# Linear attention's level products issued upwards behind the diagonals, with more steps between producer and consumer

## The chip, the cores and the metric

The kernel runs on one core of one Trainium2 chip. The metric is the device time of one execution in microseconds (us), here the median of the runs. The core's engines each work through their own instruction queue in order: TensorE (PE) multiplies, VectorE (DVE) and ScalarE (ACT) do element-wise work, GpSimd (POOL) does little here, and SyncE (SP) issues most of the DMA transfers. An instruction that waits holds back everything behind it on its engine.

## The reference

One decoder layer on 256 tokens of width 2048, in float32. The part that the change touches is the mixer:

```python
n = rms_norm(x, attn_norm_g)
proj = n @ w_in                       # 5672 columns, split into the parts below
gla_out = gla_mixer(gq, gk, gv, g_lr, g_out, ...)     # 4 heads, linear attention with decay
nsa_out = nsa_mixer(nq, kc, vc, ks, vs, kw, vw, ng, ...)   # 8 heads: compressed, selected, window
h = x + jnp.concatenate([gla_out, nsa_out], axis=-1) @ w_out
m = rms_norm(h, ffn_norm_g)
return h + (jax.nn.silu(m @ w_gate) * (m @ w_up)) @ w_down

# in gla_mixer, per head (b is the running sum of the log decay):
decay = jnp.exp(jnp.where(causal, b[:, :, :, None, :] - b[:, :, None, :, :], -jnp.inf))
scores = jnp.einsum('bhtd,bhsd,bhtsd->bhts', qi, ki, decay)
# in nsa_mixer, for the compressed keys and values:
jax.nn.silu(flat @ w1) @ w2
```

## The kernel before

**Products and side work.** The large projections are main work on PE: `proj` (the input projection, 512 columns of `w_in` at a time), `w_out_half` (the output projection, one half of its rows at a time), then the feed-forward part. Each float32 product is done as three matmuls of 512 columns (line 283) on a high and a low part of both operands; lines 137 (ACT) and 138 (DVE) split the weights into `hi` and `lo` as they arrive. Everything else is written as generators ("side work") whose `yield`s mark steps. `drive(mains, pace)` issues the main products, and for each `pace` units of them (a step of three matmuls counts 2) it advances the side work by one step. The pace is 2.5 in the stage of the change and 2 in `w_out_half(0)`. Side work stands in two queues, `urgent` first and then `later`, in which one step goes to the first item in line. `later` holds in order `gla_gate`, `gla_mix`, `compress` (put in at index 1) and `nsa_mix`. So an added `yield` in one of them delays all that comes behind it in `later` by one step of main work. `urgent` and `later` are drained after `w_out_half(0)`. A background generator, `sum_rows` (line 1042), prepares sums of the feed-forward weights on DVE. The program is a Tile program: a scheduler fixes at build time the order of the instructions on each engine, beginning from the order in which the code issues them.

**Linear attention.** `gla_mix` computes two pairs of heads. `gla_decay(hp)` prepares pair `hp`: for each of the seven `LEVELS` 1, 2, 4, ... 64 two tiles of decayed keys and queries (exponentials on ACT, lines 542 and 544; then on DVE the running sums, lines 548 and 550, and the multiplications, lines 552 and 555; level 1 has a copy on line 554), and at the end a tile `off` (lines 560 to 564) for the block of scores between the two halves of the sequence. The running sums go upwards: each level's lines 548 and 550 use what the level before left. `gla_scores(h)` does ten PE products of 128x128 for head `h` (line 581): one for each level, two on the undecayed keys and queries (`near` and `far`, whose diagonals are wanted), and one on `off`. They lie four to a PSUM bank; DVE then merges a bank's products into one score tile by masked copies (`pick`, line 576). `gla_out` (lines 604 to 622) multiplies the scores with the values and normalises.

In `gla_mix` the second pair's decay runs step by step beside the first two heads' scores:

```python
nxt = gla_decay(1)
for h in range(4):
    if h == 2:
        yield from nxt
    for _ in gla_scores(h, res[h]):
        yield
        next(nxt, None)
```

**Compression.** `compress` runs twice, for keys (`w == 0`) and values. The products of line 766 fill a bank, DVE copies it (`hs`), PE transposes it (line 210), DVE reduces it (line 773), ACT applies silu (line 774), and after five further steps PE multiplies the result with the second weights (line 779 for keys, 795 for values). ACT also copies scores of the compressed branch there: lines 638 and 829 (ACT) and 639 (DVE) split the transposed queries. `nsa_mix` follows; its outputs (`put_mix`) must be there before `w_out_half(1)`, which multiplies them.

Of the kernel before, what the change touches and what calls it, by code (L numbers as in the profile page):

```python
# [12 lines left out]
ALU = mybir.AluOpType  # L13
# [15 lines left out]
WARM = (3, 2, 1)  # L29
LINE = 256  # L30
LEVELS = (1, 2, 4, 8, 16, 32, 64)
MASKED = LEVELS[:-1]
M_UP, M_LOW = len(MASKED), len(MASKED) + 1
C_LR, C_GO, C_NQ, C_KC, C_KS, C_KW, C_NG = 2048, 2064, 3088, 4112, 4624, 5136, 5648

# [2 lines left out]
def kernel(  # L38
# [6 lines left out]
    TT, TS, STT = nc.vector.tensor_tensor, nc.vector.tensor_scalar, nc.vector.scalar_tensor_tensor  # L45
# [157 lines left out]
    ident = kp.tile([P, P], F32, name="ident")  # L203
# [187 lines left out]

    lmask = cp.tile([P, len(MASKED) + 2, P], F32, name="lmask")
    cneg = cp.tile([P, 2, P], BF16, name="cneg")
# [8 lines left out]
    def constants():  # L402
# [3 lines left out]
        affine(lmask[:, M_LOW, :], [[-1, P]], -1, 1)  # L406
        for li, l in enumerate(MASKED):

# [117 lines left out]
    def gla_decay(hp):  # L526

        e = dec[hp] = {}

        def cut(a, l):  # L530
            return a.rearrange("p b h (n r i) -> p (b h n) r i", r=2, i=l)

        def blocks(a):
            return a.rearrange("p (b n) i -> p b n i", b=2)

        f_, r_ = (dec[name].rearrange("p c s -> p (c s)").rearrange("p (g b h s) -> p g b h s", g=2, b=2, h=2)[:, hp] for name in "fr")
        k_, q_ = kk[:, hp], qq[:, hp]
        for l in LEVELS:
            e[l] = g2([2, 2, P])
            f, r, q, k, ev = (cut(a, l) for a in (f_, r_, q_, k_, e[l]))  # L540
            n = f.shape[1]
            act(ev[:, :, 1, :], f[:, :, 1, :], AF.Exp, scale=1.0 / TAU)
            if l > 1:
                act(ev[:, :, 0, :], r[:, :, 0, :], AF.Exp, scale=1.0 / TAU)
            yield
            yield
            to, ends = blocks(r[:, :, 0, :]), blocks(f[:, :, 1, l - 1:l])[:, ::-1]
            TT(to, to, ends.to_broadcast([P, 2, n // 2, l]), ALU.add)
            if 2 * l < P:
                TT(f[:, :, 1, :], f[:, :, 1, :], f[:, :, 0, l - 1:l].to_broadcast([P, n, l]), ALU.add)  # L550
            if l > 1:
                TT(ev[:, :, 0, :], ev[:, :, 0, :], k[:, :, 0, :], ALU.mult)
            else:
                nc.vector.tensor_copy(ev[:, :, 0, :], k[:, :, 0, :])
            TT(ev[:, :, 1, :], ev[:, :, 1, :], q[:, :, 1, :], ALU.mult)
            yield
            yield
        off, first_g = g2([2, 2, P]), small([2, 1])
        e["off"] = off
        TS(first_g, f_[:, 0, :, 0:1], 1.0 / TAU, None, ALU.mult)  # L560
        act(off[:, 0], r_[:, 0], AF.Exp, scale=1.0 / TAU)
        for h in range(2):
            act(off[:, 1, h], r_[:, 1, h], AF.Exp, scale=1.0 / TAU, bias=first_g[:, h])
        TT(off, off, k_, ALU.mult)
        yield

    def gla_scores(h, res):

        e, hh, hp = dec[h // 2], h % 2, h // 2
        near, far = kk[:, hp, :, hh], qq[:, hp, :, hh]  # L570
        (sc0, sc1), (sc, sof) = ((t[:, 0], t[:, 1]) for t in (g1([2, P]), g1([2, P])))
        todo = [(e[l][:, 0, hh], e[l][:, 1, hh]) for l in LEVELS[::-1]]
        todo += [(near[:, 0], far[:, 1]), (far[:, 0], near[:, 1]), (e["off"][:, 0, hh], e["off"][:, 1, hh])]

        def pick(to, m, src):
            nc.vector.copy_predicated(to, lmask[:, m, :].bitcast(mybir.dt.uint32), src)

        for at in range(0, len(todo), 4):
            p = bank()
            for j, (u, w) in enumerate(todo[at:at + 4]):  # L580
                mm(p[:, j * P:(j + 1) * P], u, w, start=True, stop=True)  # L581
                yield
            for j in range(len(todo[at:at + 4])):
                i, pl = at + j, p[:, j * P:(j + 1) * P]
                if i == 0:
                    nc.vector.tensor_copy(sc, pl)
                elif i <= len(MASKED):
                    pick(sc, len(MASKED) - i, pl)
                elif i == len(MASKED) + 1:
                    TT(sc0, pl, ident, ALU.mult)  # L590
                    pick(sc0, M_UP, sc)
                elif i == len(MASKED) + 2:
                    TT(sc1[:, ::-1], pl, ident, ALU.mult)
                    pick(sc1[:, ::-1], M_LOW, sc)
                else:
                    act(sof[:, ::-1], pl, AF.Copy)
        res["s"] = sc0, sc1, sof

    def gla_out(h, res):
# [44 lines left out]
    def gla_mix():  # L644
        res = [{} for _ in range(4)]
        yield from gla_decay(0)
        nxt = gla_decay(1)
        for h in range(4):
            if h == 2:
                yield from nxt  # L650
            for _ in gla_scores(h, res[h]):
                yield
                next(nxt, None)
            if h:
                yield from gla_out(h - 1, res[h - 1])
        for _ in range(7):
            yield
        yield from gla_out(3, res[3])
# [73 lines left out]
    def compress():  # L732

        uT = st["uT"]

        def rows_of(i):

            res = []
            for j in range(2):
                to, j0 = g4([8, P]), (i % 2 * 2 + j) * 1024  # L740
                nc.gpsimd.dma_start(to, (k_w1, v_w1)[i // 2][0, j0:j0 + 1024, :].rearrange("(j p) h -> p j h", p=P))
                res.append(to)
            return res

        nxt = rows_of(0)
        for w in range(2):
            ph = bank()
            nc.vector.memset(ph[:, :P], 0.0)
            for half in range(2):
                j0 = 16 * half  # L750
                r = nxt
                if 2 * w + half < 3:
                    nxt = rows_of(2 * w + half + 1)
                blk = g2([16, 2, NCMP])
                for h in range(2):
                    u = uT[:, w, h, j0:j0 + 240].rearrange("p (n j) -> p j n", j=16)
                    TT(blk[:, :, h, :], u, pos[:, w, j0:j0 + 16].unsqueeze(2).to_broadcast([P, 16, NCMP]), ALU.add)
                for _ in range(9):
                    yield
                for j in range(16):  # L760
                    g = 32 * (j % 4)
                    mm(ph[g:g + N2, :P], blk[:, j].rearrange("p h n -> p (h n)"), r[j // 8][:, j % 8, :], start=(half == 0 and j < 4),
                       stop=(half == 1 and j >= 12), tile_position=(0, g), skip_group_check=True)
                    if j % 16 == 15:
                        yield
            hs = g1([P])
            nc.vector.tensor_copy(hs, ph[:, :P])
            for _ in range(6):
                yield
            pt = bank()  # L770
            transpose(pt[:, :P], hs)
            hid = g1([32])
            nc.vector.tensor_reduce(hid, pt[:, :P].rearrange("p (g m) -> p m g", g=4), AX.X, ALU.add)
            act(hid, hid, AF.Silu)
            for _ in range(5):
                yield
            pk = bank()
            if w == 0:
                mm(pk[:N2, :P], hid[:, :N2], cw2[:, 0, :], start=True, stop=True)
                ss = small([1])  # L780
                junk = g1([P])
                act(junk[:N2], pk[:N2, :P], AF.Square, accum_out=ss[:N2])
                TS(ss[:N2], ss[:N2], 1.0 / 128, EPS, ALU.mult, ALU.add)
                rk = small([1])
                rsqrt_(rk[:N2], ss[:N2])
                kk = g1([P])
                TS(kk[:N2], pk[:N2, :P], rk[:N2], None, ALU.mult)
                for _ in range(25):
                    yield
                pt = bank()  # L790
                transpose(pt[:, :N2], kk[:N2, :], N2)
                TS(kcm, pt[:, :N2], kgain[:, 0:1], None, ALU.mult)
            else:
                for h in range(2):
                    mm(pk[:NCMP, h * P:(h + 1) * P], hid[:, h * NCMP:(h + 1) * NCMP], cw2[:, 1, :], start=True, stop=True)
                in_parts(vcm[0][:NCMP], vcm[1][:NCMP], pk[:NCMP, :S].rearrange("p (h d) -> p h d", h=2))
            yield

    nq, sc = {}, {}
# [573 lines left out]
```

## Time and profile before

| | |
|---|---|
| runs (us) | 1122.27, 1120.46, 1120.99; median 1120.99 |
| profiled execution (us) | 1120.81, of which span 1118.8 |
| PE busy | 1100.5 us, 98% of the span |
| DVE busy | 995.1 us, 89% |
| ACT busy | 742.0 us, 66% |
| POOL busy | 76.0 us, 7% |
| DMA | 259.61 MB, mean 232 GB/s |

A row of the profile's timeline gives the start, the duration, the engine, the source line, the operation, the tiles (output<-inputs) and their shape; a bracket at its end gives the idle time before the instruction and the instruction that ended it. Matmuls are pipelined, so the distance between two starts is what one costs, not its listed duration. "PEclk" is the share of full speed that TensorE's clock was granted. Each float32 matmul of line 581 is counted as two in the trace's counts (x14 is seven products).

### The profile page before, as it was taken

What the parts mean: (1) busy time and instruction counts of PE and PEld (TensorE: products, weight loads), DVE (VectorE), ACT (ScalarE), POOL (GpSimd) and SP (SyncE); (2) the same over time, 40 slices, a digit from 0 to 9 for tenths busy, and PEclk for the clock granted to TensorE, in tenths of its full rate; (3) what the DMA queues carried; (4) which work ended last, traced back from release to release, by engine and by line L of the source; (5) the groups of instructions that cost most, each with busy time, mean ns of one, the idle gap of its engine ahead of it and who ended that gap; (6) DMA issues with size and microseconds to landing.
All of it is one profiled execution on the core that took longest, in us unless ns stands there. A gap on an engine that the chain in (4) does not pass through costs nothing.

```text
span 1118.8 us, 14633 instructions
## 1 busy us (share of the span) xinstructions
PE 1100.5 (98%) x5298; PEld 903.7 (81%) x5298; DVE 995.1 (89%) x1277; ACT 742.0 (66%) x1009; POOL 76.0 (7%) x139
## 2 busy tenths in 40 slices
PE   9999996999999999999999999999999999999998
PEld 8878885898777887888878888888888788888886
DVE  6678779878599787998899999999999999999997
ACT  7645556544566487767586676768686776767684
POOL 5110000023110000010000000000000000000000
PEclk9999998999999999999999999999999999999999
DMA  7999984468754675686565747657665657567763
GB/s 268 340 338 363 359 282 138 157 231 302 248 213 165 242 244 177 234 306 226 174 216 194 254 160 254 226 198 242 202 215 202 230 177 257 196 237 235 239 229 113
DMA packets 124850, 259.61 MB, mean 232 GB/s; under 512 B 6709, under 2 KB 8793, under 8 KB 124778
## 3 DMA queue, kind: packets, MB, share of 16 engines
q1 hardware_dynamic: 113514, 219.86, 57.6%
q0 software_dynamic: 10368, 37.75, 9.2%
q10 hardware_dynamic: 896, 1.07, 0.3%
q8 instruction: 41, 0.67, 0.2%
q14 instruction: 31, 0.25, 0.1%
HBM read 239.78 MB, written 18.87 MB: 231 GB/s over the span
## 4 chain that ended last, share of the span: by engine, by line
PE 78%; DVE 11%; DMA 3%; ACT 3%; issue 3%; POOL 1%; ACTq 0%; SPq 0%; POOLq 0%; DVEq 0%
PE bank L283 41%; PE bank L1110 28%; DVE ftwo L639 5%; PE bank L210 3%; PE bank L1251 2%; DMA raw<-in_w_in_dram 2%; DVE lo L138 2%; DVE g L1141 1%; DMA fraw<-in_w_down_dram 1%; PE bank L909 1%; PE bank L581 1%; ACT ftwo L638 1%; PE bank L846 1%; DVE g L639 1%; DVE fsum L1142 1%
## 5 line engine op out<-in xcount | busy, mean ns | idle before, releaser
L1110 PE MATMUL bank<-ftwo,g 128*128 128x512 f32 x1848 | 432.3, 393 | 0.3 <-ACT ftwo L638 0.2
L1110 PEld LDWEIGHTS bank<-ftwo,g 128*128 128x128 f32 x1848 | 342.3, 188 | 77.4 <-DVE ftwo L639 4.3
L283 PE MATMUL bank<-hi,g 128*128 128x512 f32 (+1 forms) x1088 | 320.0, 375 | 0.1
L639 DVE TENSOR_TENSOR ftwo<-fraw,ftwo 128x1536 fp32r<-128x1536 f32 (+1 forms) x130 | 257.9, 1984 | 9.4 <-ACT ftwo L638 8.0
L638 ACT ACTIVATE ftwo<-fraw 128x1536 fp32r<-128x1536 f32 (+1 forms) x130 | 216.9, 1670 | 34.7 <-DMA fraw<-in_w_up_dram 24.7
L283 PE MATMUL bank<-ftwo,g 128*128 128x512 f32 x960 | 221.7, 391 | 0.5 <-ACT bank L1222 0.5
L283 PEld LDWEIGHTS bank<-hi,g 128*128 128x128 f32 x1088 | 192.1, 188 | 31.0 <-ACT hi L323 0.7
L283 PEld LDWEIGHTS bank<-ftwo,g 128*128 128x128 f32 x960 | 179.2, 188 | 40.3 <-ACT bank L1222 2.8
L137 ACT ACTIVATE hi<-raw 128x1024 fp32r<-128x1024 f32 (+3 forms) x124 | 130.7, 1057 | 103.9 <-PE bank L283 78.1
L283 PE MATMUL bank<-lo,g 128*128 128x512 f32 (+3 forms) x544 | 193.7, 375 | 0.2 <-DVE lo L324 0.2
L138 DVE TENSOR_TENSOR lo<-raw,hi 128x1024 fp32r<-128x1024 f32 (+3 forms) x124 | 150.2, 1218 | 37.8 <-ACT hi L137 37.1
L638 ACT ACTIVATE ftwo<-g 128x1024 fp32r<-128x1024 f32 x74 | 78.2, 1056 | 70.0 <-DVE g L1141 43.8
L283 PEld LDWEIGHTS bank<-lo,g 128*128 128x128 f32 x544 | 98.3, 188 | 15.8 <-DVE lo L324 0.6
L639 DVE TENSOR_TENSOR ftwo<-g,ftwo 128x1024 fp32r<-128x1024 f32 x74 | 90.3, 1220 | 10.7 <-ACT ftwo L638 10.7
L639 DVE TENSOR_TENSOR ftwo<-fsum,ftwo 128x1024 fp32r<-128x1024 f32 x74 | 90.2, 1219 | 0.0
L638 ACT ACTIVATE ftwo<-fsum 128x1024 fp32r<-128x1024 f32 x74 | 77.5, 1048 | 5.9 <-DVE fsum L1143 4.7
L1234 ACT COPY g<-bank 128x512 f32<-128x512 f32 x80 | 45.9, 588 | 39.9 <-PE bank L283 38.1
L1141 DVE TENSOR_TENSOR g<-fraw 128x1024 f32<-128x1024 f32 x56 | 67.5, 1219 | 0.0
L1222 ACT COPY bank<-g 128x512 f32<-128x512 f32 x80 | 45.2, 593 | 13.4 <-DVE f L1171 12.1
L638 ACT ACTIVATE g<-bank 128x512 fp32r<-128x512 f32 (+1 forms) x50 | 29.1, 593 | 32.0 <-PE bank L210 27.1
L1099 POOL DMA_DIRECT2D g<-sums x16 | 8.5, 531 | 512.0 <-DVE ftwo L639 482.9
L210 PE MATMUL bank<-ident,g 128*128 128x128 f32 (+2 forms) x214 | 39.0, 278 | 0.9 <-ACT g L478 0.5
(241 smaller groups left out, 909.3 us busy)
## 6 DMA issues: line engine op xcount, KB each, us to landing
fraw<-in_w_gate_dram SPq DMA_DIRECT2D x86, 512.0 KB, 3.9
fraw<-in_w_down_dram SPq DMA_DIRECT2D x42, 1024.0 KB, 5.0
raw<-in_w_in_dram SPq DMA_DIRECT2D x36, 1024.0 KB, 7.4
fraw<-in_w_up_dram SPq DMA_DIRECT2D x70, 512.0 KB, 4.7
sums<-g POOLq DMA_DIRECT2D x32, 512.0 KB, 6.3
raw<-in_w_out_dram SPq DMA_DIRECT2D x16, 1024.0 KB, 5.2
g<-in_w_gate_dram SPq DMA_DIRECT2D x16, 512.0 KB, 7.3
g<-in_w_up_dram SPq DMA_DIRECT2D x16, 512.0 KB, 8.3
```

What stands on the lines that cost most here:

```text
L137: act(h[:, i:i + n], r[:, k + i:k + i + n], AF.Copy)
L138: last["d"] = TT(o[:, i:i + n], r[:, k + i:k + i + n], f32(h[:, i:i + n]), ALU.subtract)
L210: return nc.tensor.transpose(o, i, ident[:n, :n])
L283: last["mm"] = mm(bk[t], a[:, k, t * P:(t + 1) * P], m[:, off:off + w], start=(first_ and k == 0 and i == 0), stop=(end and k == 3 and i = ...
L581: mm(p[:, j * P:(j + 1) * P], u, w, start=True, stop=True)
L638: act(hi, ps, AF.Copy)
L639: last["d"] = TT(lo, ps, f32(hi), ALU.subtract)
L1110: mm(banks[q], x, m, start=todo[q] == total[q], stop=todo[q] == 1)
L1141: TT(s1, r[:, 1:3], r[:, 3:4].to_broadcast([P, 2, 512]), ALU.add)
L1222: nc.scalar.copy(banks[qs[n][t]], h_sb[n][:, t, :])
L1234: nc.scalar.copy(h_sb[n][:, t, :], bs[t])
L1251: mm(bk, u, m, start=(first and i == 0), stop=(end and i == 2), skip_group_check=onto)
```

## The change

Three things. First, `gla_scores` issues `near` and `far` first, then the levels from 1 to 64, then `off`; before, it went from level 64 down to 1, then `near`, `far` and `off`. The picks follow: level 1 is copied whole, the levels 2 to 64 are picked over it, and the merge of the diagonals stands at the end. There are as many picks, copies and multiplications per head as before. Secondly, `gla_mix` takes four empty steps between the first pair's decay and head 0, and begins the second pair's decay at head 1 instead of head 0 (the rest of it still in front of head 2). Thirdly, `compress` takes nine steps instead of five between silu and the second product. Below line 644 the line numbers of the changed kernel are 4 higher (774 becomes 778, 779 783, 795 799, 1042 1046). All lines of the diff:

```diff
@@ -29,7 +29,7 @@
 WARM = (3, 2, 1)
 LINE = 256
 LEVELS = (1, 2, 4, 8, 16, 32, 64)
-MASKED = LEVELS[:-1]
+MASKED = LEVELS[1:]
 M_UP, M_LOW = len(MASKED), len(MASKED) + 1
 C_LR, C_GO, C_NQ, C_KC, C_KS, C_KW, C_NG = 2048, 2064, 3088, 4112, 4624, 5136, 5648
 
@@ -569,8 +569,8 @@
         e, hh, hp = dec[h // 2], h % 2, h // 2
         near, far = kk[:, hp, :, hh], qq[:, hp, :, hh]
         (sc0, sc1), (sc, sof) = ((t[:, 0], t[:, 1]) for t in (g1([2, P]), g1([2, P])))
-        todo = [(e[l][:, 0, hh], e[l][:, 1, hh]) for l in LEVELS[::-1]]
-        todo += [(near[:, 0], far[:, 1]), (far[:, 0], near[:, 1]), (e["off"][:, 0, hh], e["off"][:, 1, hh])]
+        todo = [(near[:, 0], far[:, 1]), (far[:, 0], near[:, 1])]
+        todo += [(e[l][:, 0, hh], e[l][:, 1, hh]) for l in LEVELS] + [(e["off"][:, 0, hh], e["off"][:, 1, hh])]
 
         def pick(to, m, src):
             nc.vector.copy_predicated(to, lmask[:, m, :].bitcast(mybir.dt.uint32), src)
@@ -583,17 +583,17 @@
             for j in range(len(todo[at:at + 4])):
                 i, pl = at + j, p[:, j * P:(j + 1) * P]
                 if i == 0:
+                    TT(sc0, pl, ident, ALU.mult)
+                elif i == 1:
+                    TT(sc1[:, ::-1], pl, ident, ALU.mult)
+                elif i == 2:
                     nc.vector.tensor_copy(sc, pl)
-                elif i <= len(MASKED):
-                    pick(sc, len(MASKED) - i, pl)
-                elif i == len(MASKED) + 1:
-                    TT(sc0, pl, ident, ALU.mult)
-                    pick(sc0, M_UP, sc)
-                elif i == len(MASKED) + 2:
-                    TT(sc1[:, ::-1], pl, ident, ALU.mult)
-                    pick(sc1[:, ::-1], M_LOW, sc)
+                elif i < 2 + len(LEVELS):
+                    pick(sc, i - 3, pl)
                 else:
                     act(sof[:, ::-1], pl, AF.Copy)
+        pick(sc0, M_UP, sc)
+        pick(sc1[:, ::-1], M_LOW, sc)
         res["s"] = sc0, sc1, sof
 
     def gla_out(h, res):
@@ -644,8 +644,12 @@
     def gla_mix():
         res = [{} for _ in range(4)]
         yield from gla_decay(0)
-        nxt = gla_decay(1)
+        for _ in range(4):
+            yield
+        nxt = iter(())
         for h in range(4):
+            if h == 1:
+                nxt = gla_decay(1)
             if h == 2:
                 yield from nxt
             for _ in gla_scores(h, res[h]):
@@ -772,7 +776,7 @@
             hid = g1([32])
             nc.vector.tensor_reduce(hid, pt[:, :P].rearrange("p (g m) -> p m g", g=4), AX.X, ALU.add)
             act(hid, hid, AF.Silu)
-            for _ in range(5):
+            for _ in range(9):
                 yield
             pk = bank()
             if w == 0:
```

In the order of the instructions on the engines, the first place is PE around head 0's scores. `hi` and `lo` of 1697 are the last weights of the projection that runs there; `g_255`, `g_261`, `g_262`, `g_263`, `g_264`, `g_265`, `g_271` are levels 1, 2, 4, 8, 16, 32, 64, `g_272` is `off`, `g_16` and `g_17` keys and queries. Before, beginning with that projection's last matmul:

```order
L283 MATMUL bank_1498<-hi_1697,g_56_365 128x512
L581 MATMUL bank_1731<-g_271_1710 128x128
L581 MATMUL bank_1731<-g_265_1688 128x128
L581 MATMUL bank_1731<-g_264_1675 128x128
L581 MATMUL bank_1731<-g_263_1663 128x128
L581 MATMUL bank_1752<-g_262_1651 128x128
L581 MATMUL bank_1752<-g_261_1639 128x128
L581 MATMUL bank_1752<-g_255_1618 128x128
L581 MATMUL bank_1752<-g_17_134,g_16_133 128x128
L581 MATMUL bank_1774<-g_16_133,g_17_134 128x128
L581 MATMUL bank_1774<-g_272_1721 128x128
L581 MATMUL bank_1787<-g_271_1710 128x128
```

and of the changed kernel, beginning with level 2 (`near`, `far` and level 1 stand eight to four rows above it, among the same projection's matmuls):

```order
L581 MATMUL bank_1737<-g_261_1639 128x128
L283 MATMUL bank_1498<-hi_1697,g_55_364 128x512
L283 MATMUL bank_1498<-lo_1698,g_55_364 128x512
L283 MATMUL bank_1498<-hi_1697,g_56_365 128x512
L581 MATMUL bank_1751<-g_262_1651 128x128
L283 MATMUL bank_1761<-hi_1765,g_24_150 128x512
L283 MATMUL bank_1761<-lo_1766,g_24_150 128x512
L283 MATMUL bank_1761<-hi_1765,g_25_151 128x512
L283 MATMUL bank_1762<-hi_1765,g_24_150 128x512
L283 MATMUL bank_1762<-lo_1766,g_24_150 128x512
L283 MATMUL bank_1762<-hi_1765,g_25_151 128x512
L581 MATMUL bank_1751<-g_263_1663 128x128
```

The ten products stood in one block behind the projection, level 64 first; now level 4 is the first that stands behind it, six matmuls of the next projection stand between levels 4 and 8, five between 8 and 16, then with eight transposes among them five and two, and `off` comes four rows behind level 64.

The second place is DVE at the end of the first pair's decay (`g_271`, `g_272` as above; `g_277` and `g_279` are the second pair's levels 1 and 2, `g_275` head 0's score tile). Before:

```order
L548 TENSOR_TENSOR g_81_570<-g_81_570,g_80_569 128x4x64
L552 TENSOR_TENSOR g_271_1710<-g_271_1710,g_16_133 128x4x64
L555 TENSOR_TENSOR g_271_1710<-g_271_1710,g_17_134 128x4x64
L554 COPY g_277_1734<-g_16_133 128x256
L564 TENSOR_TENSOR g_272_1721<-g_272_1721,g_16_133 128x512
L550 TENSOR_TENSOR g_80_569<-g_80_569 128x256
L555 TENSOR_TENSOR g_277_1734<-g_277_1734,g_17_134 128x256
L548 TENSOR_TENSOR g_81_570<-g_81_570,g_80_569 128x128x2
L552 TENSOR_TENSOR g_279_1755<-g_279_1755,g_16_133 128x128x2
L586 COPY g_275_1730<-bank_1731 128x128
L550 TENSOR_TENSOR g_80_569<-g_80_569 128x128x2
L576 COPY_PREDICATED g_275_1730<-lmask,bank_1731 128x128
```

and of the changed kernel (`g_274` and `g_275` are head 0's score tiles, `g_293` is the second pair's level 1, `g_265` level 32):

```order
L555 TENSOR_TENSOR g_265_1688<-g_265_1688,g_17_134 128x8x32
L548 TENSOR_TENSOR g_81_570<-g_81_570,g_80_569 128x4x64
L552 TENSOR_TENSOR g_271_1710<-g_271_1710,g_16_133 128x4x64
L588 TENSOR_TENSOR g_274_1735<-bank_1737,ident 128x128
L590 COPY g_275_1736<-bank_1737 128x128
L555 TENSOR_TENSOR g_271_1710<-g_271_1710,g_17_134 128x4x64
L576 COPY_PREDICATED g_275_1736<-lmask,bank_1737 128x128
L554 COPY g_293_1825<-g_16_133 128x256
L564 TENSOR_TENSOR g_272_1721<-g_272_1721,g_16_133 128x512
L576 COPY_PREDICATED g_275_1736<-lmask,bank_1751 128x128
L138 TENSOR_TENSOR lo_1850<-raw_1843,hi_1849 128x2x512
```

The second pair's decay followed at once; now the diagonals and picks of head 0 stand between, and a split of weights (line 138; `lo_1850`, numbered `lo_1884` before, where it stood amid level 8's lines) has moved behind the decay, while one multiplication of `near` (line 586) has its old place.

The third place is ACT around the first silu of `compress` (line 774, 778 in the changed kernel), with the splits of weights (line 137) and the copies of the queries (638, 829). Before:

```order
L638 ACTIVATE g_471_2768<-bank_2770 128x512
L638 ACTIVATE g_471_2768<-bank_2782 128x512
L829 COPY g_470_2767<-bank_2770 128x512
L137 ACTIVATE hi_2855<-raw_2849 128x2x512
L829 COPY g_470_2767<-bank_2782 128x512
L774 ACT_TABLE_LOAD
L774 ACTIVATE g_481_2809<-g_481_2809 128x32
```

and of the changed kernel:

```order
L638 ACTIVATE g_467_2727<-bank_2729 128x512
L638 ACTIVATE g_467_2727<-bank_2741 128x512
L833 COPY g_466_2726<-bank_2729 128x512
L833 COPY g_466_2726<-bank_2741 128x512
L137 ACTIVATE hi_2845<-raw_2839 128x2x512
L137 ACTIVATE hi_2885<-raw_2883 128x2x512
L778 ACT_TABLE_LOAD
L778 ACTIVATE g_481_2827<-g_481_2827 128x32
```

The last copy of the queries stood right in front of silu's table load; now both copies stand ahead of two splits. On PE twelve matmuls of line 283 stand between the transposition and the product that uses silu's result, thirteen before; at the second silu nine, eleven before, and one split stands between the copies and silu where none stood.

## Prediction

> **What bounds the kernel now.** I read the page first: the busy shares, and the span in 40 slices of 28 us.
>
> ```profile
> span 1118.8 us, 14633 instructions
> ...
> PE 1100.5 (98%) x5298; PEld 903.7 (81%) x5298; DVE 995.1 (89%) x1277; ACT 742.0 (66%) x1009; POOL 76.0 (7%) x139
> ...
> PE   9999996999999999999999999999999999999998
> ...
> PEclk9999998999999999999999999999999999999999
> ```
>
> PE bounds the kernel: it is idle for 1118.8 - 1100.5 = 18.3 us in all. One slice, the seventh (168 to 196 us), stands out in both rows: PE is at 6 tenths, its clock at 8. Next, the list of what PE waits for:
>
> ```profile
> PE bank L581 <- DVE g L555: 8.6, 1, 8.6
> PE bank L795 <- ACT g L774: 1.6, 1, 1.6
> PE bank L200 <- DVE g L194: 1.3, 1, 1.3
> PE bank L779 <- ACT g L774: 1.0, 1, 1.0
> ```
>
> One wait is the level products' (line 581) on the decay (line 555); two are on the compression's silu (774). The third row lies at the program's start, which the change leaves alone. So the sum is made of three waits and of the slow clock behind the first. Their places, in the timeline of PE:
>
> ```profile
> 174.60 0.39 PE L283 MATMUL bank<-hi,g 128*128 128x512 f32 x1
> 183.62 3.35 PE L581 MATMUL bank<-g 128*128 128x128 f32 x14 [8.62 <-DVE g L555]
> 186.76 1.04 PE L581 MATMUL bank<-g,g 128*128 128x128 f32 x4
> ```
>
> PE ends the projection at 174.60 + 0.39 = 175.0 and stands until 183.62. The busy time by stretches (PE, PE's weight loads, DVE, ACT, POOL, then the granted clock and the DMA share):
>
> ```profile
> 175.00:183.60 8.60, 0.00 (x0) 0.00 (x0) 8.60 (x22) 6.15 (x16) 0.00 (x0) 0.64 0.61 219
> 183.60:186.00 2.40, 2.38 (x11) 2.38 (x12) 2.21 (x7) 1.74 (x6) 0.00 (x0) 0.50 0.03 11
> 186.00:188.00 2.00, 2.00 (x13) 2.00 (x13) 1.80 (x7) 0.90 (x3) 0.00 (x0) 0.59 0.00 0
> 188.00:222.00 34.00, 34.00 (x192) 29.45 (x191) 28.50 (x73) 17.55 (x40) 1.41 (x2) 1.00 0.36 128
> 222.00:231.00 9.00, 9.00 (x76) 9.00 (x75) 7.51 (x18) 4.65 (x9) 2.86 (x3) 1.00 0.55 177
> 283.50:284.80 1.30, 0.28 (x3) 0.03 (x2) 0.46 (x1) 1.29 (x3) 0.00 (x0) 1.00 0.86 337
> 309.00:310.30 1.30, 0.10 (x1) 0.11 (x2) 1.27 (x4) 1.29 (x4) 0.00 (x0) 1.00 0.46 175
> ```
>
> DVE is busy for the whole 8.60 us in which PE stands: the decay is DVE's work, and PE waits for its last level because the old order wants that one first. Behind the wait the clock is 0.50 for 2.40 us and 0.59 for 2.00, so 2.40 x 0.50 + 2.00 x 0.41 = 2.0 us are lost too. At the two silu waits the clock stays 1.00.
>
> **Part one: the order of the levels.** No product is added or removed. When each level is there, on DVE now:
>
> ```profile
> 176.97 0.42 DVE L555 TENSOR_TENSOR g<-g,g 128x256 f32<-128x256 f32 x1
> ...
> 177.98 1.22 DVE L138 TENSOR_TENSOR lo<-raw,hi 128x1024 fp32r<-128x1024 f32 x1
> 179.11 0.42 DVE L550 TENSOR_TENSOR g<-g 128x256 f32<-128x256 f32 x1
> 179.45 0.42 DVE L555 TENSOR_TENSOR g<-g,g 128x256 f32<-128x256 f32 x1
> ...
> 183.13 0.43 DVE L555 TENSOR_TENSOR g<-g,g 128x256 f32<-128x256 f32 x1
> ...
> 183.96 0.69 DVE L564 TENSOR_TENSOR g<-g,g 128x512 f32<-128x512 f32 x1 [0.19 <-ACT g L563]
> ```
>
> These are level 4 (ready at 177.39), a split of weights, level 8 (179.87), level 64 (183.56) and `off` (184.65). I walk the new order on PE against them. Prices: a level product is 3.14 us / 7 at half clock (183.62 to 186.76), so 0.22 at full; a matmul of line 283 is 0.23 (nine of them from 306.17 to 308.22, rows below).
>
> PE now has `near`, `far` and levels 1 and 2 in front of the projection's end, so it comes to level 4 at 175.0 + 4 x 0.22 = 175.9. DVE's order is unchanged up to there: 177.4. **A wait of 1.5 us remains.** From here on six matmuls stand before level 8: PE is there at 177.4 + 0.2 + 6 x 0.23 = 179.0. On DVE the split of 1.13 us (177.98 to 179.11) moves behind the decay and a 128-column operation of some 0.2 us takes its place, so level 8 is ready 0.93 us sooner, at 178.9. Level 16 comes five matmuls later, at 180.4; level 32 nine or ten matmul prices later, at 182.6; level 64 at 183.3. DVE is ready with the last at 183.56 - 0.93 + 0.4 (two more multiplications of diagonals in front) = 183.0. All just in time, within 0.1 to 1 us. `off` is wanted at 184.1 and ready at about 184.65 - 0.93 + 0.8 (diagonals and two picks in front) = 184.5: **0.4 us remain**, 0 to 0.8.
>
> With no idle time longer than 1.6 us I take the clock as staying at 1.00, as at the silu waits (2.0 us kept).
>
> Behind that DVE is the tight engine. PE would run 8.62 + 2.0 - 1.5 - 0.4 = 8.7 us ahead of where it was, and DVE must do the same work as much earlier. Its idle time from 183.6 to 231 us, where the heads' scores end and the key stage runs, is 0.19 + 0.20 + 5.50 + 1.49 = 7.4 us. That is 1.3 us short. Some of its work there isn't wanted by PE soon (the background sums, line 1042, and weights split ahead), so I take **0.8 us** of new short waits (0 to 1.3), at the weight splits and at the later heads' levels. The split moved behind the decay was several us ahead of its use and costs nothing of its own.
>
> **Part two: four steps in front of head 0 and the later second decay.** The steps are empty; on PE they put matmuls of line 283 between decay and scores, which is the walk above. The second pair's decay is the same DVE work, begun a head later; head 2 is behind by about as much, and its cost is in the 0.8.
>
> **Part three: four more steps behind silu.**
>
> ```profile
> 283.19 1.28 ACT L774 ACT_TABLE_LOAD   x1
> 284.49 0.23 ACT L774 ACTIVATE g<-g 128x32 f32<-128x32 f32 x1
> ...
> 308.83 1.18 ACT L829 COPY g<-bank 128x512 f32<-128x512 f32 x2 [2.44 <-DVE g L639]
> 309.91 0.23 ACT L774 ACTIVATE g<-g 128x32 f32<-128x32 f32 x1
> ```
>
> ```profile
> 280.50 0.27 PE L210 MATMUL bank<-ident,g 128*128 128x128 f32 x1
> ...
> 284.77 0.41 PE L779 MATMUL bank<-cw,g 128*30 128x128 f32 x2 [1.02 <-ACT g L774]
> ...
> 306.17 0.62 PE L283 MATMUL bank<-hi,g 128*128 128x512 f32 x2
> ...
> 308.22 0.39 PE L283 MATMUL bank<-hi,g 128*128 128x512 f32 x1
> 310.19 0.61 PE L795 MATMUL bank<-cw,g 128*15 128x128 f32 x4 [1.59 <-ACT g L774]
> ```
>
> ```profile
> 308.11 1.28 DVE L639 TENSOR_TENSOR g<-bank,g 128x512 fp32r<-128x512 f32 x2
> 309.31 0.28 DVE L773 TENSOR_REDUCE g<-bank 128x32 f32<-128x128 f32 x1
> ```
>
> Silu itself is short; what is late is the queue in front of it, the query copies (829) on ACT and their partners (639) on DVE, which hold the reduction until 309.31. The added steps don't widen the distance on PE (twelve and nine matmuls of line 283 stand between transposition and product, against thirteen and eleven), but the transposition now comes later than the queries', so the copies are done when silu's turn comes. First chain: reduction 0.28, table 1.28, silu 0.23, some handing over, about 2.2 us, against 12 x 0.23 + 0.2 = 2.95. Second: no table load, 0.28 + 0.23 and one split that may stand in front (about 1.1), against 9 x 0.23 = 2.05. Both waits go: 1.02 + 1.59 = **2.6 us**. What is late next is the copy ahead of the transposition (line 771 before), which has about 1.6 us of matmuls for cover.
>
> **What is moved with it.** Sparse attention's steps stand 14 + 2 x 4 = 22 steps later in their queue. They ended 28 matmuls (6.4 us) before `w_out_half(1)`, they now end 6 (1.4 us) before it; but the first matmul that wants the last of their output stands some 24 matmuls further on. From `w_out_half(1)` on PE's order is the same. The weights of the compression (loads on POOL's queue) are asked for later, like their use; two loads of the background sums (SP's queue) pass a load of main weights. No PE wait in the list is on a DMA there. I take **0.3 us** for all of it (0 to 1.5).
>
> **The sum.** Against the profiled execution of 1120.81 us, which is 0.2 under the median of the runs: gains 8.62 + 2.0 + 2.6 = 13.2; new or remaining 1.5 + 0.4 + 0.8 + 0.3 = 3.0. Net 10.2: 1110.6 us.
>
> **The rivals.**
> (a) DVE becomes the bound of the stage. Then the gain there is no more than its idle time, 7.4 us to 231 or 5.9 to 222, and with the silu 2.6 less 0.3 the time is 1111.1 to 1112.6. For it: 8.60 us busy of 8.60, and the walk's margins of 0.1 us. [...]
> (b) Slower: sparse attention, 22 steps later, spills over the drain in front of `w_out_half(1)`. PE would then do its last score and output steps as a bare chain of DVE and ACT work. It decides from more than 12.4 us of new waits there (10.2 gained and 0.2% lost); it lost 22 x 0.23 = 5.1 us of cover, so 5.1 us is its likelier price, 1115.7, and over 1123 needs an added chain behind it.
> (c) The silu waits stay, since the PE distance is shorter than before: 2.6 us back, 1113.2.
> (d) Everything hides, DVE included: 1120.8 - 13.2 = 1107.6.
>
> **How the numbers follow.** The forecast's own case (1109 to 1112) 0.50; (a) 0.23, of it 0.06 with the clock; (c) 0.08; (d) 0.09; (b) 0.07, of it 0.03 over 1123; a wait that I don't see, with the time between 1116 and 1123, 0.03. The range 1107.4 to 1115.5 takes in (d), (a) and (c) and leaves out (b) and the last: about 1 in 10, and some for the sizes of my estimates. This kernel's measurement tells 0.2% (2.2 us) from no change, so faster means below 1118.7. Chances: faster 0.93, same 0.03, slower 0.04.
>
> **What would show it.** In the profile after: the wait of line 581 on 555 at 1 to 2 us instead of 8.6; the granted clock 1.00 from 175 to 192; no wait on silu's line over 0.5; DVE's busy share over 0.95 from 175 to 222; PE's sum of waits on splits (line 138) under 1 us; and no new wait in front of the drain. The prediction is wrong if a wait over 3 us stands at any level, if the clock shows 0.5 again, or if `w_out_half(1)` starts with a wait on attention's outputs.

## The result, and the profile after

The changed kernel takes 1110.59 us (median of 4 runs, 1109.58 to 1111.69) against 1120.83 us (median of 4) for the kernel before: ratio 0.9906, 95% interval 0.9889 to 0.9924, so 10.2 us faster. The forecast was 1110.6. The profiled execution took 1109.58 us, 1.0 us under that median; the one of before 1120.81.

The page of the changed kernel, its busy shares and the two rows of slices that stood out before:

```profile
span 1107.9 us, 14624 instructions
...
PE 1097.7 (99%) x5298; PEld 900.7 (81%) x5298; DVE 991.5 (89%) x1277; ACT 741.5 (67%) x1009; POOL 74.0 (7%) x139
...
PE   9999999999999999999999999999999999999998
...
PEclk9999999999999999999999999999999999999999
```

The hole in the seventh slice is gone in both rows. PE's idle time fell from 18.3 to 1107.9 - 1097.7 = 10.2 us, its busy time by 2.8 us; together they are the span's 10.9. Of the 2.8, 2.0 are what PE lost behind the wait, where it ran at half clock from 183.62 to 187.64 us. Another 0.7 lie at the program's start, which the change doesn't touch: four matmuls of line 200 took 1.77 us before and 1.03 now. What PE waits for now:

```profile
PE bank L283 <- ACT hi L323: 1.3, 1, 1.3
PE bank L581 <- DVE g L555: 1.3, 1, 1.3
PE bank L200 <- DVE g L194: 1.3, 1, 1.3
PE bank L283 <- ACT bank L1226: 1.0, 1, 1.0
PE bank L210 <- DVE g L814: 0.5, 1, 0.5
PE bank L210 <- DVE g L714: 0.3, 1, 0.3
```

The 8.6 us on the decay are 1.3; silu's line (778) is not in the list. The first and third row are the program's start; the first, where the split of line 323 waited for a weight transfer, is not in the list of before, and in the kernels below it goes from none to 1.1 us. Row four is in the feed-forward part. The wait at level 4, in PE's timeline, and the three stretches behind it (columns as before):

```profile
175.40 0.39 PE L283 MATMUL bank<-hi,g 128*128 128x512 f32 x1
177.08 0.49 PE L581 MATMUL bank<-g 128*128 128x128 f32 x2 [1.29 <-DVE g L555]
```

```profile
175.00:177.40 2.40, 1.11 (x7) 0.63 (x6) 2.40 (x7) 2.13 (x4) 0.00 (x0) 1.00 0.90 256
177.40:184.50 7.10, 7.10 (x41) 5.65 (x40) 6.76 (x22) 5.86 (x15) 0.00 (x0) 1.00 0.40 156
184.50:188.00 3.50, 3.50 (x25) 3.17 (x25) 3.50 (x13) 2.24 (x5) 0.00 (x0) 1.00 0.35 97
```

From 177.4 to 188 us PE doesn't stand for a moment, with the clock at 1.00. Over the whole of the heads' scores, the same stretch of before and then of the changed kernel:

```profile
175.00:222.00 47.00, 38.38 (x211) 33.84 (x212) 41.11 (x107) 26.34 (x61) 1.41 (x2) 0.89 0.38 133
```

```profile
175.00:222.00 47.00, 45.42 (x272) 39.16 (x272) 44.88 (x118) 29.44 (x66) 3.92 (x5) 1.00 0.53 174
```

PE goes from 38.38 to 45.42 us of 47, DVE from 41.11 to 44.88: DVE's spare time there is down from 5.9 to 2.1 us.

### The profile page after: what moved, and what is told of

It is laid out like the page before. It is cut to its first block, busy times and chain, and to the rows that moved or that the text cites. A ratio compares the mean times of both kernels' runs of the same rounds, so it can differ in the third digit from the quotient of the medians.

```text
span 1107.9 us, 14624 instructions
## 1 busy us (share of the span) xinstructions
PE 1097.7 (99%) x5298; PEld 900.7 (81%) x5298; DVE 991.5 (89%) x1277; ACT 741.5 (67%) x1009; POOL 74.0 (7%) x139
## 4 chain that ended last, share of the span: by engine, by line
PE 83%; DVE 6%; DMA 6%; issue 2%; ACT 2%; SPq 0%; POOL 0%; ACTq 0%; POOLq 0%; DVEq 0%
PE bank L283 39%; PE bank L1114 35%; DMA raw<-in_w_in_dram 3%; PE bank L210 3%; DMA g<-in_w_up_dram 2%; PE bank L1255 2%; DVE ftwo L639 2%; DVE lo L138 2%; PE bank L913 1%; PE bank L850 1%; ACT hi L137 1%; PE bank L581 1%; DMA fraw<-in_w_down_dram 1%; DVE g L1145 0%; DVE g L1046 0%
```

## The experiments

Each kernel was timed against the kernel before on the same chip. The differences are of medians; ratios are to before.

| kernel | us | before | difference | ratio, 95% interval |
|---|---|---|---|---|
| the change | 1110.59 | 1120.83 | -10.2 | 0.9906, 0.9889 to 0.9924 |
| upward order alone | 1119.11 | 1120.82 | -1.7 | 0.9988, 0.9979 to 0.9997 |
| four steps alone | 1119.10 | 1120.82 | -1.7 | 0.9985, 0.9976 to 0.9994 |
| nine silu steps alone | 1120.54 | 1120.41 | +0.1 | 0.9997, 0.9989 to 1.0005 |
| change, second decay early | 1113.00 | 1120.82 | -7.8 | 0.9931, 0.9918 to 0.9943 |
| change, five silu steps | 1110.44 | 1120.82 | -10.4 | 0.9912, 0.9898 to 0.9925 |
| change, downward order | 1119.05 | 1120.41 | -1.4 | 0.9988, 0.9980 to 0.9997 |
| change, no steps | 1115.71 | 1120.41 | -4.7 | 0.9955, 0.9942 to 0.9967 |
| change, three steps | 1109.21 | 1119.83 | -10.6 | 0.9900, 0.9887 to 0.9914 |
| change, six steps | 1112.25 | 1119.83 | -7.6 | 0.9928, 0.9916 to 0.9941 |
| change, eight steps | 1113.15 | 1120.41 | -7.3 | 0.9934, 0.9920 to 0.9947 |
| change, two splits behind the decay | 1110.44 | 1119.83 | -9.4 | 0.9916, 0.9902 to 0.9929 |
| eight steps, less DVE work | 1111.55 | 1119.83 | -8.3 | 0.9928, 0.9914 to 0.9942 |

**The upward order alone.** To the kernel before, only `MASKED` and `gla_scores` of the change:

```diff
+        todo = [(near[:, 0], far[:, 1]), (far[:, 0], near[:, 1])]
+        todo += [(e[l][:, 0, hh], e[l][:, 1, hh]) for l in LEVELS] + [(e["off"][:, 0, hh], e["off"][:, 1, hh])]
...
```

> The upward order alone: near, far and the levels from 1 to 64, no empty steps in front of head 0, the second decay beside heads 0 and 1 as before, five steps behind silu. My theory: PE reaches level 4 at the same time as in the changed kernel and then finds levels 4, 8, 16, 32 and 64 in a row with nothing between them; it waits at each of the five, 1.0 to 1.5 us each (about 6 us in all, ready at the pace of DVE, level 64 at 182.6 us). No single wait is longer than 1.6 us, so the clock stays at 1.00 and the time falls by 8.6 - 6 + 2.0 = about 4.8 us, to 1116. The silu waits stay (2.6 us in all). Rival: the clock goes by the busy share of a stretch, not by an unbroken wait; it falls here too, and the gain is 2.5 to 3 us (about 1118).

PE's level products that waited, and the busy time in stretches:

```profile
177.16 0.49 PE L581 MATMUL bank<-g 128*128 128x128 f32 x2 [1.29 <-DVE g L555]
179.00 0.49 PE L581 MATMUL bank<-g 128*128 128x128 f32 x2 [1.35 <-DVE g L555]
180.34 0.80 PE L581 MATMUL bank<-g 128*128 128x128 f32 x2 [0.85 <-DVE g L555]
181.68 0.80 PE L581 MATMUL bank<-g 128*128 128x128 f32 x2 [0.54 <-DVE g L555]
182.78 0.77 PE L581 MATMUL bank<-g 128*128 128x128 f32 x2 [0.30 <-DVE g L555]
```

```profile
175.00:179.00 4.00, 1.36 (x8) 0.69 (x6) 3.79 (x11) 3.55 (x8) 0.00 (x0) 1.00 0.45 181
179.00:182.50 3.50, 2.08 (x6) 1.30 (x6) 3.50 (x11) 2.23 (x7) 0.00 (x0) 0.56 0.00 0
182.50:184.00 1.50, 1.22 (x5) 1.25 (x6) 1.50 (x6) 1.16 (x4) 0.00 (x0) 0.50 0.00 0
184.00:186.00 2.00, 2.00 (x7) 1.61 (x7) 2.00 (x8) 1.28 (x3) 0.00 (x0) 0.50 0.00 0
```

Five waits in a row, as the theory had it, 4.3 us together. But the clock fell, to 0.56 from 179 to 182.5 us and to 0.50 from there to 186, though no wait is longer than 1.35 us; in the 4.00 us ahead of it PE was busy for 1.36. So the clock did what the rival had said. The gain is 1.7 us by the medians, which is under the rival's 2.5 to 3 as well; the profiled execution alone (1117.92) is 2.9 under that of before. The order alone breaks one wait into five; it puts no other work between the levels that are late.

**The four steps alone**, in the downward order:

```diff
         yield from gla_decay(0)
+        for _ in range(4):
+            yield
```

> The four empty steps alone, in the downward order. My theory: level 64 is still the first product wanted, no main matmul comes between the projection's end and it, so the wait of 8.6 us, the slow clock and the time stay: 1120.8, within 1 us. Rival: the steps themselves bring the cover; then the wait falls by some of 4 steps' matmuls (four to five of them, 1 us) and the time with it, to 1119 or less.

The wait is 8.68 us and the clock 0.50 behind it, until about 188.5 (0.98 from 188 to 200); the 1.7 us are outside my "within 1 us". Seven products instead of ten follow the wait, but main matmuls run at half clock in their place (0.43 us from one start to the next, from 186.36 to 186.79, against 0.23 at full clock), so nothing is gained by that. Silu's two waits are 1.3 and 0.6 us instead of 1.6 and 1.0, with the compression four steps later. That is 0.7 of the 1.7; where the rest comes from is not shown. The rival's cover of the wait isn't there.

**The second decay early again.** `nxt = gla_decay(1)` in front of the heads, the rest as changed.

> The changed kernel with the second pair's decay beside heads 0 and 1 again (begun at head 0). My theory: the decay is the same DVE work and is needed at head 2 in both; PE's wait at level 4 stays 1.3 us, 'off' is at most 0.5 us later, and the time is 1110.6 to 1111.5. Rival: DVE is the bound of this stage, and the second decay in front of head 0's picks holds back score tiles and weight splits: 2 to 4 us slower, 1113 to 1115, with waits of PE on splits or picks.

2.4 us slower than the changed kernel by the differences: my theory fell, the rival holds. The wait at level 4 is the same 1.29; the new one, in PE's timeline:

```profile
196.60 0.50 PE L283 MATMUL bank<-lo,g 128*128 128x512 f32 x1 [1.45 <-DVE lo L138]
```

A weight split is late on DVE, behind head 0's picks and the second decay that now stand together ahead of it. There are also waits of 0.6 each on silu's line, on line 769 (the compression's copy) and in attention, with these ten steps further forward, where the changed kernel has 0.3 and 0.5 on lines 714 and 814. So the 2.4 us are the price of the place as a whole; the split's wait is 1.45 of it.

**Five silu steps instead of nine**, the rest as changed:

```diff
-            for _ in range(9):
+            for _ in range(5):
```

> The changed kernel with five steps behind silu instead of nine. My theory: the silu waits went because the whole compression stands later against the queries' copies, not because of the added steps; seven matmuls (1.6 us) between transposition and product at the second silu still cover the 1.0 us from the transposition to silu's end, twelve at the first as in the changed kernel: no silu wait, 1110.6 within 0.7. Rival: the nine steps carry the 2.6 us, or half of them: 1112 to 1113.2, with waits on silu's line.

The same time. The first silu wait is gone as in the changed kernel; at the second, with seven matmuls behind the transposition instead of nine, 0.4 us come back, too little to be seen in the time.

**Without the steps**, the rest as changed:

> The changed kernel without the four empty steps. The run with the upward order alone showed five waits in a row (4.3 us, none over 1.4) with the clock at 0.56 and 0.50 from 179 to 186 us. My theory: the steps and the order work only together: without the steps the levels again stand in a row, the waits come to about 4.3 us instead of 1.3, and the clock falls and costs another 2 to 3 us; 5 to 6 us slower than the changed kernel, about 1116. Rival: the parts add, so that it loses what the steps alone brought (1.7 us): 1112.3, with the clock at 1.00.

```profile
PE bank L581 <- DVE g L555: 4.6, 5, 1.4
```

Five waits and the slow clock again (0.72, 0.50, 0.50 and 0.67 in the stretches from 179 to 188 us); 5.5 us slower than with the steps by the differences, as the theory had it. The steps bring 1.7 us alone and 5.5 with the rest of the change. Silu's line is not in this kernel's list of waits.

**Nine silu steps alone**, to the kernel before:

> The nine steps behind silu alone. My theory: they do nothing here either, since the queue in front of silu (query copies on ACT and DVE) sets the waits: both silu waits stay (13 and 9 matmuls now stand between transposition and product, 13 and 11 before), 1120.8 within 0.8. Rival: the steps hide the waits: 2 us faster, 1118.5.

No change in the time. The waits are 1.0 and 0.8 us: the second was 1.6, so the added steps do take half of that one, which the rival had, but it can't be seen in the time.

**The downward order with all the rest**: four steps, late second decay, nine silu steps.

> The changed kernel with the downward order: empty steps, later second decay and nine silu steps only. My theory: the wait of 8.7 us on level 64 and the slow clock stay; the silu waits (2.6 us) go because the compression stands 14 steps later, and the three products that no longer follow the wait run at full clock (0.7): about 1117.5. Rival: the shift of the compression brings nothing by itself: 1119 as with the four steps alone.

```profile
PE bank L581 <- DVE g L555: 8.9, 2, 8.6
PE bank L200 <- DVE g L194: 1.2, 1, 1.2
PE bank L210 <- DVE g L814: 0.8, 1, 0.8
PE bank L210 <- DVE g L622: 0.6, 1, 0.6
```

The time is the rival's, the mechanism in half mine: silu's line has left the list, but 1.4 us of waits on line 814 (the queries' copy) and 622 (a head's output) stand in it instead. The large wait is whole. Without the order, the rest of the change is worth 1.4 us.

**Eight steps instead of four**, the rest as changed:

> The changed kernel with eight empty steps instead of four. Level 2 now comes behind twelve matmuls of the next projection, so that the wait of 1.3 us at level 4 goes; by the walk levels 32 and 64 then wait some 0.3 us each. My theory: about 0.7 to 1 us come out at the level products, but DVE, busy all the time there, gives part of it back at a weight split or a later head; 1109.6 to 1110.6. Rival: attention's steps, four more behind, now end at the drain, and a bare chain there costs 1 to 3 us: 1111.5 to 1113.5.

Both texts missed in part. The time is the rival's, the cause mine: there is no wait at any level, and none over 0.2 us in front of the drain, but

```profile
PE bank L210 <- DVE g L814: 2.7, 2, 1.8
PE bank L283 <- DVE lo L138: 1.6, 2, 1.1
```

and behind the waits on line 814 (1.80 and 0.88 us, ending at 269.23 and 270.44) the clock falls once more:

```profile
266.00:269.00 3.00, 1.43 (x7) 0.85 (x5) 3.00 (x6) 1.78 (x2) 0.83 (x2) 1.00 0.91 266
269.00:271.00 2.00, 0.89 (x4) 0.64 (x5) 2.00 (x6) 0.00 (x0) 0.00 (x0) 1.00 0.87 348
271.00:273.00 2.00, 2.00 (x10) 1.68 (x9) 1.85 (x3) 0.65 (x2) 1.19 (x1) 0.65 0.17 27
273.00:275.00 2.00, 2.00 (x6) 1.52 (x6) 0.59 (x3) 0.55 (x1) 1.46 (x2) 0.50 0.85 294
```

2.00 x 0.35 + 2.00 x 0.50 = 1.7 us are lost by it. That stands against 2.9 us less gained than with four steps. DVE is busy all of 266 to 271: the compression's block sums (line 761), moved back by the steps, now stand among the queries' copies.

**Six steps and three steps.**

> The changed kernel with six empty steps. Level 4 now stands ahead of eleven matmuls and the rest behind them. My theory: the wait at level 4 stays near 1.3 to 1.5 us, none follows at the levels; the split that stood behind the decay is back in it, and as with eight steps head 0's picks and splits come late: a wait of about 1 us at a split and some at the queries' copies, 1111.5 to 1113. Rival: six steps is between four and eight in the levels' waits only, 1110 to 1110.6.

> The changed kernel with three empty steps. Level 4 again stands behind the projection's end with six matmuls behind it, then five, as with four; level 32 comes some three matmuls sooner. My theory: the gain hangs on main matmuls standing between the levels, not on the number of steps, so three do nearly as well: wait at level 4 1.3 us, up to 0.5 at level 32, clock 1.00, 1110.6 to 1111.6. Rival: the gain goes down evenly with the steps (5.1 us for four): 1111.9.

Six steps:

```profile
PE bank L581 <- DVE g L555: 1.5, 1, 1.5
PE bank L210 <- DVE g L814: 1.3, 2, 0.9
PE bank L210 <- DVE g L622: 0.9, 1, 0.9
```

and 2.6 us less gained than with four. The time, the wait at level 4 and those on the queries' copies are my theory's; its wait on a split did not come, and one on a head's output (622) did. Three steps are as good as four, with 1.3 us at level 4 and nothing else in the stage over 0.4; both texts had expected 1110.6 us or more (on this chip the kernel before, too, takes 1.0 us less than in the runs for the change):

```profile
PE bank L581 <- DVE g L555: 1.3, 1, 1.3
PE bank L200 <- DVE g L194: 1.3, 1, 1.3
PE bank L210 <- DVE g L714: 0.4, 1, 0.4
```

So the gain isn't even in the steps: 4.7 us without any, 10.6 with three, 10.2 with four, 7.6 with six, 7.3 with eight. Three and four have six matmuls behind level 4 and five behind level 8, where the kernel without steps has none. With six and eight no level behind 4 waits either, and what is lost stands in waits on DVE further on. Three and four can't be told apart.

**Two splits behind the decay.** The two subtractions of line 138 for the weights after next (`lo_1846`, `lo_1850`) are bound behind `off`, by a count in `split`:

```diff
+        op = TT(off, off, k_, ALU.mult)
+        if hp == 0:
+            last["off"], last["held"] = op, 4
...
+                with behind(last["off"] if 0 < held <= 2 else None):
```

> The changed kernel with two splits of weights on DVE (the pair for the projection after next) bound behind the first pair's 'off'. One of them stood between levels 2 and 4 (1.13 us). My theory: level 4 is ready as PE comes to it and the wait of 1.3 us goes; the splits are done about when PE wants them (186.5 us), so up to 1.3 us are gained, 1109.3 to 1110.6. Rival: DVE is the bound up to 200 us, so that what is taken from the level's wait comes back as a wait on the splits: 1111 to 1112.

No wait on the levels is left, and nothing is gained against the changed kernel. In the list (lines below 138 stand 3 to 5 lower in this kernel: 286 is 283, 213 is 210, 141 is 138, 819 is 814, 627 is 622):

```profile
PE bank L213 <- DVE g L819: 0.8, 1, 0.8
PE bank L286 <- DVE lo L141: 0.6, 1, 0.6
PE bank L213 <- DVE g L627: 0.5, 1, 0.5
PE bank L213 <- DVE g L719: 0.4, 1, 0.4
```

The 1.3 us came back as a wait on a split, on a head's output, and some more on the queries' copy. The time lies in my range, what happened is the rival's.

**Eight steps with less DVE work.**

```diff
-            TT(ev[:, :, 1, :], ev[:, :, 1, :], q[:, :, 1, :], ALU.mult)
+            if hp == 0:
+                TT(ev[:, :, 1, :], ev[:, :, 1, :], q[:, :, 1, :], ALU.mult)
```

> The kernel with eight empty steps, with the multiplications of the second pair's levels by the queries left out (seven on DVE, 0.335 us each, 2.3 us in all). My theory: at eight steps it is DVE's load that is late at the weight split behind head 0 (a wait of 1.1 us at 195 us); with 2.3 us less DVE work around it that wait goes, and the time falls by 1 to 2 us, to 1111 to 1112. Rival: the order of DVE's queue, not its load, holds the split: the wait stays and the time is 1113 within 0.7.

The kernel leaves these multiplications out, so it doesn't compute the layer and serves for its time alone.

```profile
PE bank L210 <- DVE g L815: 2.7, 2, 1.8
PE bank L200 <- DVE g L194: 1.3, 1, 1.3
PE bank L210 <- DVE g L715: 1.1, 2, 0.6
```

The splits are gone from the list (1.6 us with eight steps), the wait on the queries' copy (815, which was 814) is as it was, the clock falls once more (its mean is 0.97 from 250 to 311 us, as with eight steps), and the gain is 8.3 us instead of 7.3: 1 us of 2.3 taken from DVE, by differences whose intervals overlap. The waits speak for DVE's load as what held the splits back; the time alone doesn't show it.

## Why the prediction was right, and where its reasons weren't

- **The level wait.** Put at 1.5 us behind the walk, measured 1.29; `off` was put at 0.4 and has no wait. This was the larger part of the gain, and it needs the order and the steps together: 1.7 us each alone, 4.7 for all but the steps, 1.4 for all but the order, 10.2 for the whole.
- **The clock.** "With no idle time longer than 1.6 us I take the clock as staying at 1.00" came out (2.0 us kept), but the reason was wrong, and the changed kernel, with a single wait at the levels, does not put it to the test: the upward order alone lost the clock with waits of 1.35 us and less. What differs is how much PE worked around the waits. From 175 to 179 us PE was busy for 2.71 of the 4.00 us in the changed kernel, and its clock stayed at 1.00; with the upward order alone it was busy for 1.36, and the clock was 0.50 from about 179.4 on. Before the change the clock fell 2.40 us into the wait of 8.62. The chances give (a) 0.06 "with the clock"; the clock did not fall.
- **DVE as the tight engine.** Put at 0.8 us of short waits; in the stage there is one of 0.29 (line 714), and 0.51 on line 814 further on. DVE is busy 44.88 of 47 us, 95%. It was the right engine to watch: the kernels with six and eight steps, with the early second decay and with the moved splits each find most of their new waits behind it. Rival (a), DVE as the bound, named the right engine, but its limit of 7.4 us did not hold: the rows of the stage give 8.6 + 2.0 - 1.3 - 0.3 = 9.0.
- **The later second decay.** This is the step that failed in the part on it: "the same DVE work, begun a head later; ... its cost is in the 0.8". Its place is worth 2.4 us, 1.45 of them since, begun early, it stands in front of a weight split.
- **The silu waits.** They went (2.6 us), and, as argued, not by the added steps: 10.4 us are gained with five. The ten steps of the later decay seem to do most of it: without the four empty steps the waits are gone too, without the later decay 0.6 us stay, and with the four alone the waits went from 2.6 to 1.9. The later decay by itself was not tried. "The added steps don't widen the distance on PE" holds against the kernel before, but not against the change with five steps, where seven matmuls stand there at the second silu and not nine. Rival (c) has nothing for it.
- **Sparse attention, 22 steps later.** Put at 0.3 us; no wait over 0.2 us stands in front of the drain, at eight steps neither. Rival (b) has nothing for it.
- **The sum.** By the rows: 8.6 + 2.0 + 2.6 - 1.3 - 0.3 - 0.5 = 11.1 us; the profiled executions differ by 11.2, the medians by 10.2. The near agreement of the first two is partly chance, since the rows at the program's start are left out (1.3 us of wait more, 0.7 of work less). That the forecast fell on the median to 0.1 us is more than its working can claim: its 3.0 us of new waits were 2.1 in the rows, and the changed kernel's runs spread over 2 us.

## What to carry to other kernels

When a consumer wants several products of a chain, issue them in the order in which the chain yields them, and see to it that other work stands between them: either half alone moves little here. Then stop: here the engine behind the chain was 95% busy with four steps, more lead came back as waits on its next pieces of work, and the best lead was found by trying a few. And when idle time is broken into pieces, look at the granted clock, not only at the pieces.

## What the hardware showed that I had not expected

The granted clock fell without any long wait. With the upward order alone, five waits of 1.29, 1.35, 0.85, 0.54 and 0.30 us with single products between them had it at 0.50 from about 179.4 to 186.2 us. With eight steps, two of 1.80 and 0.88 us with one product between them had it at 0.50 from about 271.6 to 275.0, though PE was busy 2.32 of the 5.00 us around them (266 to 271). Single waits of 1.02, 1.29 and 1.59 us between full work left it at 1.00.

PE's busy time in 4.00 us around such waits, with the clock that was granted in them and behind them:

| kernel | stretch (us) | PE busy (us) | share | clock in it | clock behind it |
|---|---|---|---|---|---|
| before | 175 to 179 | 0.00 | 0% | 0.80 | 0.50 until 187.6 |
| no steps | 175 to 179 | 1.17 | 29% | 1.00 | 0.72 to 182.5, then 0.50 |
| eight steps | 267 to 271 | 1.32 | 33% | 1.00 | 0.50 from 271.6 |
| upward order alone | 175 to 179 | 1.36 | 34% | 1.00 | 0.50 from 179.4 |
| before, second silu wait | 307 to 311 | 2.41 | 60% | 1.00 | 1.00 |
| six steps | 175 to 179 | 2.48 | 62% | 1.00 | 1.00 |
| the change | 175 to 179 | 2.71 | 68% | 1.00 | 1.00 |
| before, first silu wait | 282 to 286 | 2.98 | 75% | 1.00 | 1.00 |

In the first four rows the clock fell, in the last four it did not. What it goes by, over which length and from which share, the rows don't show, and PE's busy time is partly modelled.

The same wait can cost more or less. With nine silu steps alone the wait of 8.65 us ends at 183.59, as before the change (8.62, 183.62), but the clock was still 1.00 from 177.4 to 179, where before the change it was 0.50, and it was at half until about 189.2 (0.50 from 186 to 188, 0.95 from 188 to 200) instead of 187.6. So about 5.6 us of work ran at half clock instead of 4.0. With the upward order alone the executions whose mean granted clock was 0.996 or 0.997 took 1117.60 to 1118.39 us, and those with 0.995 took 1119.11 to 1121.12.
